# Up-projections in one stream: seven-product column groups in five pairs instead of one, and VectorE's placement copies on GpSimd

## The chip, the cores and the metric

The kernel runs on one core of a Trainium2 chip. The metric is the device time of one execution in microseconds. Five engines work in parallel, each through its own instructions in their order: TensorE (PE, with its weight loads as PEld), VectorE (DVE), ScalarE (ACT), GpSimd (POOL) and SyncE (SP), which issues nearly all loads of weights. Work on different engines meets at semaphores.

## The reference

A trunk of two layers on 256 positions of width 2048, all in float32. Layer 0 mixes positions with grouped-query attention, layer 1 with dilated window attention and a position bias. Each mixer is followed by a gated MLP, which is the part that the change touches most:

```python
def conv_ffn(h, w_up, conv_w, conv_b, w_down):     # D_FF = 5632
    u = h @ w_up                                   # 2048 -> 2 * 5632
    u = depthwise_conv3(u, conv_w) + conv_b        # along the positions
    gate, val = jnp.split(u, 2, axis=-1)
    return (jax.nn.silu(gate) * val) @ w_down      # 5632 -> 2048
```

(The convolution is written out here as a name; before each mixer and each MLP stands an RMS norm, behind each a residual add.)

## The kernel before

**Products.** All weights are float32. A block of a weight (`raw`, 128 rows by 2 x 512 columns, one load of 512 KB) is split by ScalarE into a rounded part `wh` and by VectorE into the rest `wl` (lines 130 and 131, in `split_raw`). The activations are split in the same way once. A product is then three matmuls: xh by wh, xl by wh, xh by wl. Every matmul that matters here has 512 columns. A regular unit of work (a "c unit") takes one block and both halves of the 256 positions: 2 row tiles x 2 halves x 3 = 12 matmuls.

**Seven products.** For some column groups (512 of the 2048 rows of the weight, over a pair of 512-column stripes), the 2 x 2 block product is made with seven products of sums of blocks instead of eight products of blocks. A "P unit" is one of those products: 2 row tiles x 3 = 6 matmuls, and it too needs one split of one block. Four regular c units (48 matmuls, four splits) become seven P units (42 matmuls, seven splits). Four of the seven products need a sum of weight blocks, and three or four of them a sum of activations, the "forms" (`make_forms`). The partial results M1, M5, M6, M7 are copied or added by ScalarE and VectorE into two tiles `ms`, and the results of the accumulators are added to them at the end.

**The MLP.** The 5632 columns are 11 stripes of 512 for the gate and 11 for the value; stripe p of both is a pair. Pairs 0 to 5 are the first half, 6 to 10 the second; each half is projected up and then at once down (`w_down` rows of that half), so a layer has up, down, up, down. `project` runs one stripe with four column groups of `feed` (16 c units a pair); pair 0 weaves its two stripes so that the last column groups of the input can still be made. Only the first pair of the second half (pair 6) goes through `seven`, with column group 0 as seven P units and the remaining twelve c units woven between. Its forms are made during the down-projection before it. In `feed` the second matmul of a block already reads `wl` (line 156 behind 155).

**Behind a stripe** runs the generator `up_post`: scale and copy out of PSUM (line 629), a 32 x 32 transpose on VectorE (630), sixteen copies that place the turned blocks (`place_blocks`, lines 395, 397 and 399; `PLACE = "pava"`: four on GpSimd, eight on ScalarE, four on VectorE), the convolution (638 to 644), then silu, the product with the gate and the splits (or forms) for the down-projection. A generator advances by one piece at each `step()`, which is called after each c unit; up to two generators advance at a time. The order of instructions on each engine is then set by a scheduler from the order of the code, in which the splits of weights are moved ahead by a fixed number of instructions (`AHEAD`).

**Buffers.** Six `raw` blocks, three pairs of `wh`/`wl` (four in the down-projection), eight PSUM banks. GpSimd issues the transfers that add one block onto another (`accum_op`), which the down-projection uses for one or two of its sums of blocks (line 251).

## Time and profile before

| | |
|---|---|
| median of 3 runs | 2234.61 us (2234.25 to 2234.72) |
| the profiled execution | 2234.03 us, its span 2232.2 us |
| TensorE busy | 2218.3 us, 99% |
| VectorE busy | 1848.1 us, 83% |
| ScalarE busy | 1564.8 us, 70% |
| GpSimd busy | 349.1 us, 16% |
| weight blocks split | 873 |

The busy time of TensorE is not the sum of its matmuls' durations: they overlap, one starting about every 0.227 us while each is shown with 0.39 us. What a matmul costs is therefore read from the distance of two starts, and a stall from a distance above it. By the first matmuls of each, the four stages of the MLP begin in layer 0 at 262.8 us (up), 526.3 (down), 650.3 (up) and 868.3 (down, to 974.4), and in layer 1 at 1514.8, 1777.2, 1901.1 and 2118.8 us (to the end).

### The profile page before, as it was taken

What the parts mean: (1) busy time and instruction counts of PE and PEld (TensorE: products, weight loads), DVE (VectorE), ACT (ScalarE), POOL (GpSimd) and SP (SyncE); (2) the same over time, 40 slices, a digit from 0 to 9 for tenths busy, and PEclk for the clock granted to TensorE, in tenths of its full rate; (3) what the DMA queues carried; (4) which work ended last, traced back from release to release, by engine and by line L of the source; (5) the groups of instructions that cost most, each with busy time, mean ns of one, the idle gap of its engine ahead of it and who ended that gap; (6) DMA issues with size and microseconds to landing.
All of it is one profiled execution on the core that took longest, in us unless ns stands there. A gap on an engine that the chain in (4) does not pass through costs nothing. (4 is left out here: it accounts for less than half of the span.)

```text
span 2232.2 us, 29276 instructions
## 1 busy us (share of the span) xinstructions
PE 2218.3 (99%) x9997; PEld 1834.7 (82%) x9997; DVE 1848.1 (83%) x2543; ACT 1564.8 (70%) x2411; POOL 349.1 (16%) x508
## 2 busy tenths in 40 slices
PE   9999999999999999999999999999999999999998
PEld 7888888888888888888888888888888888888886
DVE  6777778889998888879887978796887899888896
ACT  7665677777557777667876777575777765677764
POOL 2210212211001011111340213010111100011111
PEclk9999999999999999999999999999999999999999
DMA  8444657766776656766656565555666677566675
GB/s 302 163 148 151 204 189 210 242 200 193 235 217 205 199 193 193 246 204 205 214 176 191 167 207 179 189 197 185 196 193 194 199 226 227 199 197 191 222 236 161
DMA packets 129670, 448.99 MB, mean 201 GB/s; under 512 B 17664, under 2 KB 18432, under 8 KB 129520
## 3 DMA queue, kind: packets, MB, share of 16 engines
q1 hardware_dynamic: 119744, 425.64, 57.9%
q0 software_dynamic: 9344, 20.92, 4.9%
q8 instruction: 78, 1.28, 0.2%
q14 instruction: 72, 0.59, 0.1%
q10 hardware_dynamic: 432, 0.56, 0.1%
HBM read 438.11 MB, written 6.29 MB: 199 GB/s over the span
## 5 line engine op out<-in xcount | busy, mean ns | idle before, releaser
L131 DVE TENSOR_TENSOR wl<-raw,wh 128x1024 fp32r<-128x1024 f32 x873 | 1069.3, 1234 | 267.3 <-ACT wh L130 263.6
L130 ACT ACTIVATE wh<-raw 128x1024 fp32r<-128x1024 f32 x873 | 916.3, 1057 | 453.6 <-PE acc L157 157.6
L156 PE MATMUL acc<-wl,xh 128*128 128x512 f32 x1664 | 648.9, 390 | 1.4 <-DVE wl L131 0.9
L155 PE MATMUL acc<-wh,xh 128*128 128x512 f32 x1664 | 648.9, 390 | 0.5 <-ACT wh L166 0.5
L157 PE MATMUL acc<-wh,xh 128*128 128x512 f32 x1664 | 648.0, 389 | 0.0
L156 PEld LDWEIGHTS acc<-wl,xh 128*128 128x128 f32 x1664 | 312.5, 188 | 68.7 <-DVE wl L131 4.1
L155 PEld LDWEIGHTS acc<-wh,xh 128*128 128x128 f32 x1664 | 312.4, 188 | 64.7 <-ACT wh L166 0.9
L157 PEld LDWEIGHTS acc<-wh,xh 128*128 128x128 f32 x1664 | 312.4, 188 | 64.3
L320 PE MATMUL acc<-wh,ah 128*128 128x512 f32 x730 | 284.6, 390 | 0.4 <-DVE h L578 0.3
L322 PE MATMUL acc<-wh,al 128*128 128x512 f32 x730 | 284.3, 389 | 0.0
L395 POOL COPY u<-t 32x256 f32<-32x256 f32 x176 | 110.4, 627 | 805.3 <-DVE t L630 797.2
L325 PE MATMUL acc<-wl,ah 128*128 128x512 f32 x730 | 205.1, 390 | 0.6 <-DVE wl L131 0.6
L320 PE MATMUL acc<-wh,xh 128*128 128x512 f32 x416 | 162.9, 392 | 0.2 <-DVE h L578 0.2
L322 PE MATMUL acc<-wh,xh 128*128 128x512 f32 x416 | 162.0, 389 | 0.0
L320 PEld LDWEIGHTS acc<-wh,ah 128*128 128x128 f32 x730 | 137.0, 188 | 29.8 <-DVE h L578 1.3
L325 PEld LDWEIGHTS acc<-wl,ah 128*128 128x128 f32 x730 | 136.7, 188 | 30.2 <-DVE wl L131 2.0
L322 PEld LDWEIGHTS acc<-wh,al 128*128 128x128 f32 x730 | 137.1, 188 | 28.3
L397 ACT ACTIVATE u<-t 32x256 f32<-32x256 f32 x352 | 147.6, 419 | 17.2 <-DVE t L630 9.4
L325 PE MATMUL acc<-wl,xh 128*128 128x512 f32 x416 | 113.1, 390 | 0.0
L320 PEld LDWEIGHTS acc<-wh,xh 128*128 128x128 f32 x416 | 78.1, 188 | 16.8 <-DVE h L578 0.8
L325 PEld LDWEIGHTS acc<-wl,xh 128*128 128x128 f32 x416 | 78.0, 188 | 16.2
L322 PEld LDWEIGHTS acc<-wh,xh 128*128 128x128 f32 x416 | 78.1, 188 | 16.0
(271 smaller groups left out, 2487.1 us busy)
## 6 DMA issues: line engine op xcount, KB each, us to landing
raw<-in_w_up_dram SPq DMA_DIRECT2D x352, 512.0 KB, 4.5
raw<-in_w_down_dram SPq DMA_DIRECT2D x176, 512.0 KB, 5.0
raw<-in_w_b_dram SPq DMA_DIRECT2D x144, 512.0 KB, 4.5
raw<-in_w_bo_dram SPq DMA_DIRECT2D x48, 512.0 KB, 4.4
raw<-in_w_a_dram SPq DMA_DIRECT2D x40, 512.0 KB, 4.5
raw<-in_w_ao_dram SPq DMA_DIRECT2D x32, 512.0 KB, 3.7
raw<-in_w_down_dram POOLq DMA_DIRECT2D x17, 512.0 KB, 6.2
raw<-in_w_a_dram SPq DMA_DIRECT2D x16, 256.0 KB, 6.4
```

The source lines that it names most:

```text
L130: nc.scalar.activation(wh, r, AF.Copy)
L131: nc.vector.tensor_tensor(wl, r, wh.bitcast(F32), ALU.subtract)
L155: nc.tensor.matmul(accs[m], xh, wh[:, j, :], start=st, stop=False)
L156: nc.tensor.matmul(accs[m], xh, wl[:, j, :], start=False, stop=False)
L157: nc.tensor.matmul(accs[m], xl, wh[:, j, :], start=False, stop=sp)
L320: nc.tensor.matmul(acc[k], xh, wh[:, j, :], start=k in fresh, stop=False)
L322: nc.tensor.matmul(acc[k], xl, wh[:, j, :], start=False, stop=False)
L325: nc.tensor.matmul(acc[k], xh, wl[:, j, :], start=False, stop=last[k] == i and j == 1)
L395: nc.gpsimd.tensor_copy(dst, src)
L397: nc.scalar.activation(dst, src, AF.Copy)
```

## The change

The loops over the pairs of a half, `project`, `project_woven` and `seven` for one pair, are replaced by one function `stream`, which makes a list of units for all pairs of a half. Pairs 1, 3, 5, 7 and 9 (`SEVEN_UP`) take their column group 0 as seven P units, and these are woven between the last seven c units of the pair ahead of them. Pair 6 becomes a regular one. Of the four sums of weight blocks of such a group, two are made by VectorE (`add`) and two by transfers that GpSimd issues (`onto`). In a unit, the matmuls with `wh` (eight of a c unit, four of a P unit) all come ahead of those with `wl`. The forms are made at the start of each half (`half_forms`) and kept in tiles of the pools that the down-projection's inputs take later.

`PLACE` becomes `"papa"`: the four copies of VectorE go to GpSimd, which then has eight. `up_post` waits two steps more between the copies and the convolution. `bias_lines`, a side task of layer 0, gets other tiles, and one fixed PSUM bank for its six small matmuls.

**TensorE at the end of pair 0 in layer 0.** `acc` are accumulators in PSUM, `xh` activations, `fm` forms. Before, the value stripe of pair 0 ended, and pair 1 began, with c units one behind the other, each in the order wh, wl, wh:

```order
L155 MATMUL acc_2641<-wh_2876,xh_2430 128x512
L156 MATMUL acc_2641<-wl_2877,xh_2430 128x512
L157 MATMUL acc_2641<-wh_2876,xh_2430 128x512
L155 MATMUL acc_2642<-wh_2876,xh_2430 128x512
L156 MATMUL acc_2642<-wl_2877,xh_2430 128x512
L157 MATMUL acc_2642<-wh_2876,xh_2430 128x512
```

And with the change:

```order
L434 MATMUL acc_2785<-wl_2952,xh_2430 128x512
L434 MATMUL acc_2785<-wl_2952,xh_2433 128x512
L434 MATMUL acc_2786<-wl_2952,xh_2430 128x512
L434 MATMUL acc_2786<-wl_2952,xh_2433 128x512
L427 MATMUL acc_2973<-wh_2969,fm_2647 128x512
L428 MATMUL acc_2973<-wh_2969,fm_2648 128x512
L427 MATMUL acc_2973<-wh_2969,fm_2647 128x512
L428 MATMUL acc_2973<-wh_2969,fm_2648 128x512
L434 MATMUL acc_2973<-wl_2970,fm_2647 128x512 x2
L427 MATMUL acc_2785<-wh_2982,xh_2528 128x512
L428 MATMUL acc_2785<-wh_2982,xh_2528 128x512
```

A P unit of pair 1, with six matmuls on the form 2647/2648, now stands between two c units of pair 0, whose four matmuls with `wl` come at their end.

**VectorE where the two accumulators of a stripe with seven products are added to `ms`.** Before (pair 6, the value stripe), with the split `wl_6508` that is next:

```order
L131 TENSOR_TENSOR wl_6472<-raw_6446,wh_6471 128x1024
L642 SCALAR_TENSOR_TENSOR cg_6300<-u_2617,cw_2605,cg_6300 128x256 x2
L644 SCALAR_TENSOR_TENSOR cg_6300<-u_2617,cw_2605,cg_6300 128x256 x2
L425 TENSOR_TENSOR ms_6073<-acc_6076,ms_6073 128x512
L426 TENSOR_TENSOR ms_6073<-acc_6077,ms_6073 128x512
L131 TENSOR_TENSOR wl_6508<-raw_6503,wh_6507 128x1024
```

With the change (pair 1, the gate stripe):

```order
L132 TENSOR_TENSOR wl_3325<-raw_3322,wh_3324 128x1024
L762 SCALAR_TENSOR_TENSOR cv_2875<-u_2618,cw_2605,cv_2875 128x256
L797 TENSOR_TENSOR cv_2875<-cg_2873,cv_2875 128x512
L442 TENSOR_TENSOR ms_2886<-acc_2942,ms_2886 128x512
L442 TENSOR_TENSOR ms_2886<-acc_3116,ms_2886 128x512
L132 TENSOR_TENSOR wl_3350<-raw_3347,wh_3349 128x1024
```

The two adds stand in both directly ahead of a split, and wait for the end of a stripe; less of other work is ahead of them now, and there are ten such stripes a layer instead of two.

**GpSimd in the first pairs of layer 0.** `u` is the placed stripe, `scr` a scratch of the side task. Before:

```order
L1147 CAST lh<-rs 128x768
L395 COPY u_2617<-t_2871 32x8x32 x4
L395 COPY u_2618<-t_3029 32x8x32 x4
L395 COPY u_2617<-t_3229 32x8x32 x4
L395 COPY u_2618<-t_3433 32x8x32 x4
L1161 DMA scr_97<-lnt 4x32x512 x4
```

With the change:

```order
L1257 CAST lh_3688<-rs 128x128
L373 DMA raw_2884<-in_w_up_dram 128x1024
L511 COPY u_2617<-t_2877 32x8x32 x8
L373 DMA raw_2936<-raw_2967 128x1024
L511 COPY u_2618<-t_3107 32x8x32 x8
L511 COPY u_2617<-t_3275 32x8x32 x8
L511 COPY u_2618<-t_3445 32x8x32 x8
```

Eight copies where there were four, and the two adding transfers of pair 1 (line 373) now stand among them, the second behind the eight copies of a stripe.

The diff, cut to its core:

```diff
-PLACE = "pava"
+SEVEN_UP = (1, 3, 5, 7, 9)
+PLACE = "papa"
...
+    def stream(w, lhs, forms, pairs, is_seven, held, gate_done, value_done, new_sums):
+        units, left = [], {}
+        for p in pairs:
+            order = WOVEN if held and p == pairs[0] else [(c, k) for c in range(2) for k in range(4)]
+            if p in is_seven:
+                units[-7:] = [u for v, f in zip(units[-7:], ORDER_D) for u in (v, ("P", p, 0, f))]
+            units += [("c", p, k, 2 * c + i) for c, k in order for i in range(2) if k or p not in is_seven]
+            left.update({(p, n): 8 for n in range(2)})
+            if p in is_seven:
+                left.update({(p, 0): 8, (p, 1): 7})
+        sets = [(bank_at[0] + 2) % 4, bank_at[0]]
+        acc, sums, blocks = {}, {}, {}
+
+        def where(p, k):
+            if (p, k) not in acc:
+                n, m = {"11": (0, 0), "21": (0, 1), "12": (1, 0), "22": (1, 1)}.get(k, (None, None))
+                if n is None:
+                    i = {"M1": 4, "M5": 5, "M6": 6, "M7": 7}[k]
+                elif p in is_seven and n:
+                    i = 4 + m
+                else:
+                    i = sets[n] + m
+                acc[p, k] = bank(i, "acc")
+                return acc[p, k], True
+            return acc[p, k], False
+
+        def block(p, b):
+            if b not in blocks:
+                blocks[b] = load_raw(w, p + NPAIR * (int(b[1]) - 1), 0, int(b[0]) - 1)
+            return blocks[b]
+
+        def add(b, src):
+            with tc.high_priority(offset=AHEAD):
+                nc.vector.tensor_tensor(blocks[b], blocks[b], blocks[src], ALU.add)
+
+        def onto(b, src):
+            nc.gpsimd.dma_start(blocks[b].rearrange("p a c -> p (a c)"), src, accum_op=ALU.add)
+
+        def fetch(p, f):
+            if f == 1:
+                block(p, "11")
+                block(p, "12")
+            elif f == 2:
+                add("11", "12")
+                onto("12", w[p + NPAIR, 0][:, 1024:])
+            elif f == 5:
+                add("22", "11")
+                onto("21", block(p, "22").rearrange("p a c -> p (a c)"))
+            b = {1: "11", 2: "21", 3: "22", 5: "11", 6: "22", 7: "12", 4: "21"}[f]
+            return b, block(p, b)
+
+        def product_done(p, f):
+            (k0, k1), (q0, q1) = sums[p]
+            k = {1: "M1", 5: "M5", 6: "M6", 7: "M7"}[f]
+            t = acc.pop((p, k))
+            if f in (1, 5):
+                nc.scalar.activation(k0 if f == 1 else q1, t, AF.Copy)
+            elif f == 6:
+                nc.vector.tensor_tensor(q0, t, k0, ALU.add)
+            else:
+                nc.vector.tensor_tensor(k1, t, q0, ALU.add)
+                nc.vector.tensor_tensor(q0, q0, q1, ALU.add)
+                nc.vector.tensor_tensor(q1, k1, q1, ALU.add)
+
+        for i, (kind, p, kg, f) in enumerate(units):
+            if held and i == 2 * held:
+                drain()
+            if kind == "c":
+                b, r = None, load_raw(w, p + NPAIR * (f // 2), kg, f % 2)
+                n, ks = f // 2, (("11", "21"), ("12", "22"))[f // 2]
+            else:
+                b, r = fetch(p, f)
+                n = {2: 0, 4: 0, 3: 1}.get(f)
+                ks = ({1: "M1", 2: "11", 3: "12", 4: "21", 5: "M5", 6: "M6", 7: "M7"}[f],)
+                if f == 1:
+                    sums[p] = new_sums()
+            free = kind == "c" or f in (5, 6, 7, 4)
+            wh, wl = split_raw(r, free)
+            if kind == "P" and free:
+                blocks.pop(b)
+            todo = []
+            for j in range(2):
+                for m, k in enumerate(ks):
+                    if kind == "c":
+                        x = at(lhs[4 * kg + 2 * (f % 2) + j], m)
+                    else:
+                        x = forms[f]
+                        x = x[j] if isinstance(x, list) else [t[:, j * P:(j + 1) * P] for t in x]
+                    todo.append((*where(p, k), *x, j))
+            for t, fresh, xh, xl, j in todo:
+                nc.tensor.matmul(t, xh, wh[:, j, :], start=fresh, stop=False)
+                nc.tensor.matmul(t, xl, wh[:, j, :], start=False, stop=False)
+            todo.sort(key=lambda u: ([u[0] is acc[p, k] for k in ks].index(True), u[4]))
+            if n is not None:
+                left[p, n] -= 1
+            ends = n is None or left[p, n] == 0
+            for t, fresh, xh, xl, j in todo:
+                nc.tensor.matmul(t, xh, wl[:, j, :], start=False, stop=ends and j == 1)
+            if n is None:
+                product_done(p, f)
+            elif ends:
+                a = [acc.pop((p, k)) for k in (("11", "21"), ("12", "22"))[n]]
+                if p in is_seven:
+                    s = sums[p][n]
+                    for m in range(2):
+                        nc.vector.tensor_tensor(s[m], a[m], s[m], ALU.subtract if n else ALU.add)
+                    a = s
+                    if n:
+                        sums.pop(p)
+                        sets.reverse()
+                (gate_done, value_done)[n](a, p)
+            if kind == "c" or f in (1, 5, 7, 4):
+                step()
+        bank_at[0] = sets[1]
...
                 place_blocks(u.rearrange("p j (m t) -> p j m t", m=2), t, PLACE)
                 yield
+                yield
+                yield
                 for hh in range(2):
...
+            kept, up_forms = {}, ({}, {})
+
+            def form_tiles(hf):
+                fm = [tuple(wp.tile([P, NT], F32R, tag=f"a{c}{k}", name=nm("fm")) for c in "hl")
+                      for k in range(26 + 2 * hf, 30)]
+                if hf == 0:
+                    t = [wp.tile([P, 2, 512], F32, tag=t, name=nm("xs")).rearrange("p a c -> p (a c)")
+                         for t in ("wh9", "wl9")]
+                else:
+                    t = [t[:, :1024] for t in ut]
+                    f2 = fp.tile([P, 4, NT], F32R, tag="tT", name=nm("ff"))
+                    fm += [(f2[:, 0], f2[:, 1]), (f2[:, 2], f2[:, 3])]
+                return *(v.rearrange("p (j c) -> p j c", j=4) for v in t), fm
+
+            def half_forms(hf):
+                for _ in range(4 * hf):
+                    yield
+                yield from make_forms(up_forms[hf], hT, 0, partial(form_tiles, hf))
+                if hf:
+                    zero_edges()
...
+                def gate_done(a, p, hf=hf, p0=p0, slots=slots, forms=forms, new_form=new_form, cs=cs):
...
+                    cs[p] = [[fp.tile([P, 2, NT], F32, tag=t, name=nm(t), bufs=3) for _ in range(2)]
+                             for t in ("cg", "cv")]
+                    start(up_post(a, p, cs[p][0]))
...
+                def value_done(a, p, p0=p0, slots=slots, forms=forms, cs=cs):
+                    cg, cv = cs.pop(p)
...
-                    if hf == 1 and p == p0:
-                        sums = [wp.tile([P, 2, 512], F32, tag=t, name=nm("ms")) for t in ("wh9", "wl9")]
-                        c = [("c", k, 2 * n + i) for n in range(2) for k in kgs[1:] for i in range(2)]
-                        units = c[:2]
-                        for i, f in enumerate(ORDER):
-                            units += [("P", 0, f)] + c[2 + i:3 + i] * (i < 5)
-                        units += c[7:]
...
-                        seven(w_up[l], p, NPAIR + p, hT, lambda kg: first_forms, units,
-                              [[t[:, i] for i in range(2)] for t in sums], gate_ready, value_ready)
-                        continue
-                    cg, cv = new_tiles()
-                        va = project_woven(w_up[l], p, NPAIR + p, hT, WOVEN, 4, gate_done)
-                    else:
-                        start(up_post(project(w_up[l], p, hT, kgs), p, cg))
-                        va = project(w_up[l], NPAIR + p, hT, kgs)
+                    start(up_post(a, NPAIR + p, cv, after))
...
+                start(half_forms(hf))
+                stream(w_up[l], hT, up_forms[hf], range(p0, p1), SEVEN_UP, 4 * (hf == 0), gate_done, value_done,
+                       lambda: [[t[:, i] for i in range(2)] for t in
+                                [wp.tile([P, 2, 512], F32, tag=t, name=nm("ms")) for t in ("wh9", "wl9")]])
...
-                if hf == 0:
-                    start(first_half_forms())
...
+        oh = [wp.tile([P, NT], F32R, tag=f"a{c}{k}", name=nm("oh")) for k in (24, 25) for c in "hl"]
...
+            t = bank(7, "ps")
+            for j, i in enumerate(cols):
+                nc.tensor.matmul(t[:, j * NT:(j + 1) * NT], lh.rearrange("p a r -> p (a r)"), oh[i],
+                                 start=True, stop=True)
```

More of the change, by code (lines that the diff above doesn't have):

```diff
@@ L699, in glu_forms @@
                 put(3, s4)
-            kgs = list(range(4))
             for hf, (p0, p1) in enumerate(HALVES):
@@ L710, in ffn @@
                 wide.append(1)
-                for p in range(p0, p1):
+                cs = {}
+                def gate_done(a, p, hf=hf, p0=p0, slots=slots, forms=forms, new_form=new_form, cs=cs):
                     if p - p0 in SKG[hf]:
@@ L725, in ffn, with after @@
                         slots.update({4 * (p - p0) + j: new_form() for j in range(4)})
-                    def new_tiles():
-                        return ([fp.tile([P, 2, NT], F32, tag=t, name=nm(t), bufs=3) for _ in range(2)]
-                                for t in ("cg", "cv"))
-                    def after(hh, cg, cv, slots=slots, forms=forms, kg=p - p0):
+                    if p == 0:
+                        taps()
+                    cs[p] = [[fp.tile([P, 2, NT], F32, tag=t, name=nm(t), bufs=3) for _ in range(2)]
[3 more added lines that the diff above has]
+                    cg, cv = cs.pop(p)
+                    def after(hh, kg=p - p0):
                         if kg in forms:
@@ new lines, in bias_lines @@
+        of = lp.tile([P, 2, 512], F32, tag="tT", name="of").rearrange("p a c -> p (a c)")
+        oh = [wp.tile([P, NT], F32R, tag=f"a{c}{k}", name=nm("oh")) for k in (24, 25) for c in "hl"]
+        rb = lp.tile([P, 32], F32, name="rb")[:, :24]
+        rs = lp.tile([P, 32], F32R, name="rs")[:, :24]
+        nc.gpsimd.memset(rb, 0.0)
+        nc.gpsimd.memset(rb[32:33, :], -1e30)
+        for i in range(2):
+            nc.gpsimd.dma_start(of[64 * i:64 * i + 64], onehot[:64])
+            nc.gpsimd.dma_start(rb[64 * i:64 * i + 32, :], rel_bias)
```

70 lines of the change are left out of this document (20 added, 50 removed).

## The prediction, made before the changed kernel ran

> **What bounds the kernel now.** I read the page first, then the distances between starts on TensorE, then who keeps TensorE waiting, then the busy time of every engine stage by stage.
>
> ```profile
> span 2232.2 us, 29276 instructions
> PE 2218.3 (99%) x9997; PEld 1834.7 (82%) x9997; DVE 1848.1 (83%) x2543; ACT 1564.8 (70%) x2411; POOL 349.1 (16%) x508
> PEclk9999999999999999999999999999999999999999
> 299.95 0.39 PE L157 MATMUL acc<-wh,xh 128*128 128x512 f32 x1
> ...
> 305.85 0.39 PE L156 MATMUL acc<-wl,xh 128*128 128x512 f32 x1
> PEld acc L156 <- DVE wl L131: 4.1, 8, 0.8
> PEld acc L320 <- DVE h L578: 2.1, 4, 0.7
> PEld acc L325 <- DVE wl L131: 2.0, 4, 0.7
> ```
>
> The clock is full throughout. Between the two matmuls shown lie 26 starts: 5.90 / 26 = 0.227 us from one to the next. That is the cost of one matmul of 512 columns, not the 0.39 us that it is shown with. The last three rows are the largest waits of TensorE's weight loads over the whole span: 8.2 us. So the time is the number of matmuls times 0.227 us, and whoever wants a shorter time must remove matmuls without making TensorE wait. The other engines matter only through such waits.
>
> ```profile
> 262.80:526.30 263.50, 263.50 (x1171) 218.20 (x1170) 212.32 (x321) 195.13 (x302) 50.81 (x83) 1.00 0.68 211
> 526.30:650.30 124.00, 123.41 (x542) 101.18 (x541) 117.57 (x129) 77.01 (x90) 8.08 (x12) 1.00 0.75 224
> 650.30:868.30 218.00, 217.41 (x955) 178.72 (x954) 184.09 (x269) 161.59 (x248) 23.11 (x36) 1.00 0.61 197
> ```
>
> These are three stages of layer 0 (up, down, up). After the length come the busy times of PE, PEld, DVE, ACT and POOL. VectorE is busy for 81%, 95% and 84%, ScalarE for 74%, 62% and 74%. VectorE is thus the engine that can become late first, and its fullest stage is a down-projection with six groups of seven products, 42 P units.
>
> **What is removed: 48 matmuls.** Per pair and column group, four c units of 12 matmuls become seven P units of 6: 48 become 42. Each layer has five such pairs instead of one, so 2 x 4 x 6 = 48 matmuls go: 48 x 0.227 = 10.9 us. The side task's six small matmuls keep their columns (two of 512 become four of 256). No load of a weight goes or comes on SyncE's queue: the four blocks of the group are loaded once either way.
>
> **What is added on VectorE.** The groups that carry the prices:
>
> ```profile
> L131 DVE TENSOR_TENSOR wl<-raw,wh 128x1024 fp32r<-128x1024 f32 x873 | 1069.3, 1234 | 267.3 <-ACT wh L130 263.6 <-PE ps L521 0.5 <-issue 0.2
> L399 DVE COPY u<-t 32x256 f32<-32x256 f32 x176 | 64.7, 368 | 5.9
> L277 DVE TENSOR_TENSOR raw<-raw,raw 128x1024 f32<-128x1024 f32 x40 | 49.3, 1234 | 2.3 <-DMA raw<-in_w_up_dram 1.8
> L420 DVE TENSOR_TENSOR ms<-acc,ms 128x512 f32<-128x512 f32 x8 | 5.5, 684 | 0.0
> L130 ACT ACTIVATE wh<-raw 128x1024 fp32r<-128x1024 f32 x873 | 916.3, 1057 | 453.6 <-PE acc L157 157.6 <-PE acc L322 137.9 <-DMA raw<-in_w_down_dram 40.6
> L341 DVE TENSOR_TENSOR fm<-u,fm 128x256 fp32r<-128x256 f32 x4 | 1.7, 426 | 0.0
> ```
>
> A group of seven costs VectorE three more splits (3 x 1.234), two sums of blocks (2 x 1.234; the other two go to transfers), and eight adds of partial results (8 x 0.684): 11.6 us. The forms of a half are some twelve instructions of 256 columns, 12 x 0.426 = 5.1 us. What goes are four copies a stripe, 4 x 0.368 = 1.5 us. Up, first half: 3 x 11.6 + 5.1 - 12 x 1.5 = +21.9 us on 212.3, in a stage that is 4.1 us shorter: 90%. Second half: 11.6 more for the second group, 2.5 less for the two sums that pair 6 made on VectorE, 14.7 less for ten stripes: -5.6 us, 82%. ScalarE gets 3 x 1.057 and two copies of partial results a group and stays under 80%.
>
> Inside a woven stretch I compared more closely. From the first split of a P unit to the last stand 12 further splits (14.8 us), the two sums (2.5), four adds (2.7) and, by the order of VectorE in pairs 6 and 7, other work of about 3 us: 23 us, while TensorE has six c units and six P units, 108 matmuls or 24.5 us. For pair 1 the same count gives about 24 us against 23 to 24. So the stretches are nearly balanced, and not beyond what the down-projection does with 95%. There the weight loads waited for `wl` and for accumulators as follows (520 to 640 us, whose groups are the six):
>
> ```profile
> PEld acc L325 <- DVE wl L131: 1.0, 2, 0.7
> PEld acc L320 <- DVE h L578: 0.7, 1, 0.7
> ```
>
> 1.7 us for six groups, 0.28 us each. That is the price I take for each of the ten new groups: +2.8 us. The bounds: nothing at all, or what the old group of pair 6 cost in its place:
>
> ```profile
> 698.52 0.39 PE L155 MATMUL acc<-wh,xh 128*128 128x512 f32 x1
> 699.27 0.50 PE L156 MATMUL acc<-wl,xh 128*128 128x512 f32 x1 [0.36 <-DVE wl L131]
> 699.61 0.39 PE L157 MATMUL acc<-wh,xh 128*128 128x512 f32 x1
> ...
> 731.95 0.39 PE L155 MATMUL acc<-wh,xh 128*128 128x512 f32 x1
> 732.38 0.50 PE L156 MATMUL acc<-wl,xh 128*128 128x512 f32 x1
> 732.72 0.39 PE L157 MATMUL acc<-wh,xh 128*128 128x512 f32 x1
> 696.80 0.68 DVE L425 TENSOR_TENSOR ms<-acc,ms 128x512 f32<-128x512 f32 x1
> 697.40 0.68 DVE L426 TENSOR_TENSOR ms<-acc,ms 128x512 f32<-128x512 f32 x1
> 698.00 1.22 DVE L131 TENSOR_TENSOR wl<-raw,wh 128x1024 fp32r<-128x1024 f32 x1
> ```
>
> Distances of 0.75, 0.34, 0.43 and 0.34 instead of 0.227 are 0.95 us lost, once a layer. The cause is in the last rows: the two adds wait for the end of the stripe, and the split behind them is late, because the very next matmul of the new block reads `wl`. This group is dissolved: -1.9 us for both layers. In the new order the same adds stand ahead of a split, but eight matmuls with `wh` come first, so `wl` is due 7 x 0.227 = 1.6 us later than before. That covers the 0.5 us of the first stall, and is why I stay with the lower price. If this cover is not enough, all ten groups cost 0.95.
>
> **What moves to GpSimd.**
>
> ```profile
> L395 POOL COPY u<-t 32x256 f32<-32x256 f32 x176 | 110.4, 627 | 805.3 <-DVE t L630 797.2
> 722.36 2.77 POOL L395 COPY u<-t 32x256 f32<-32x256 f32 x4 [18.04 <-DVE t L630]
> 722.15 1.18 DVE L131 TENSOR_TENSOR wl<-raw,wh 128x1024 fp32r<-128x1024 f32 x1
> 723.25 1.16 DVE L341 TENSOR_TENSOR al<-st,ah 128x256 fp32r<-128x256 f32 x2
> 724.44 0.38 DVE L399 COPY u<-t 32x256 f32<-32x256 f32 x1
> 724.85 1.36 DVE L131 TENSOR_TENSOR wl<-raw,wh 128x1024 fp32r<-128x1024 f32 x1
> 726.24 0.28 DVE L399 COPY u<-t 32x256 f32<-32x256 f32 x1
> L251 POOL DMA_DIRECT2D raw<-in_w_down_dram x17 | 14.9, 876 | 188.5 <-DVE raw L255 79.8 <-ACT wh L130 73.8 <-DMA raw<-in_w_down_dram 34.9
> raw<-in_w_down_dram POOLq DMA_DIRECT2D x17, 512.0 KB, 6.2
> raw<-raw POOLq DMA_DIRECT2D x5, 512.0 KB, 6.6
> ```
>
> Eight copies take 8 x 0.627 = 5.0 us instead of 2.5, still behind each other and ahead of the convolution of the stripe. The two added steps, at one per c unit (12 x 0.227 = 2.7 us), give them 5.4 us; no one waits for the stripe until its column group is due in the down-projection, behind several c units and P units. Cost on the path: nothing, hidden by the next pair's matmuls; without that cover 2.5 us at the end of a half, four times. The rows at 722 show that the copies do slow VectorE: two instructions of 0.42 us took 1.16, a split 1.36 instead of 1.23, a copy 0.38 instead of the 0.28 of those beside no GpSimd work; together 0.56 us for four copies. Four more a stripe put 12 x 0.56 = 6.7 us on VectorE in the first half: 93%. This is at the level of the down-projection, whose price I use.
>
> [...]
>
> The transfers that add a block have GpSimd for issuer, so each stands behind any copies ahead of it. For the sum needed by product 7, from its issue at product 2 lie four c and four P units (16.3 us); copies, issue, landing and split take 5.0 + 0.9 + 6.2 + 2.3 = 14.4 us. For product 4 the way is three and three (12.2 us) against 14.8 us, if eight copies stand right ahead. VectorE works up to two units (4 us) ahead of TensorE, so even this is just in time, and in the order of GpSimd only pair 1 of each layer has the copies there. Cost taken: nothing; bound: 2.6 us a group.
>
> **The sum.** 2234.0 (the profiled execution) - 10.9 - 1.9 + 2.8 = 2224.0. The median of the three runs is 0.6 us above that execution, so 2224.6; I write 2224.5.
>
> **Rivals.** (1) *Every group stalls like the old one*: VectorE's adds still hold up the splits. 2234.6 - 10.9 - 1.9 + 10 x 0.95 = 2231.3. For it: the same adds ahead of the split, 90% in the first half. Against it: the 1.6 us, and the rows of the down-projection. (2) *The adding transfers come late*, in every group, as product 4 waits behind GpSimd's queue: 2234.6 - 12.8 + 10 x 2.6 = 2247.8, slower. It decides from 1.3 us a group. Against it: a lead of two units, and where the down-projection uses the same transfers they were not waited for by TensorE. (3) *GpSimd's copies stop VectorE for their whole length*: 22 stripes a layer x 4 x 0.627 = 55 us. The two up stages of a layer would need 396.4 + 21.9 - 5.6 + 55 = 468 us of VectorE, at the 95% that it reached at most 493 us, where they now last 481.5: 2234.6 + 2 x 11 = 2257. [...] The row of 1.36 us speaks against it.
>
> **Chances.** The forecast 0.77 (its own range 2221.5 to 2228), rival 1 0.15, rival 2 0.05, rival 3 0.03. The lower end is the sum without any new stall, 2221.8. The range reaches to rival 1, 2231: it leaves out rivals 2 and 3, half of rival 1 and a little of the forecast. A measurement of this kernel tells 0.2%, 4.5 us, from no change, so faster means under 2230.1: nearly all of the forecast and a third of rival 1, 0.82; same: the rest of rival 1 and little of 2, 0.11; slower 0.07.
>
> **What would show it.** TensorE's busy share stays at 99%, starts 0.227 us apart, and the up stages of a layer shorten by about 4 us in the first half and by 2 in the second; splits go from 873 to 897; VectorE's copies `u<-t` are gone and GpSimd has 352. Right about the stalls: TensorE's waits for `wl` in the up stages stay under 3 us for both layers, and none is for an adding transfer. Rival 1 shows as `wl` waits of about 1 us at the end of each stripe with seven products; rival 2 as ScalarE's `wh` waiting on a `raw` transfer from GpSimd, with TensorE behind it; rival 3 as splits of 1.6 us and more wherever GpSimd copies. The forecast is wrong if TensorE loses more than 0.8 us a group.

## The result

The changed kernel takes 2274.02 us (median, 2272.05 to 2275.1), the kernel before 2234.66 beside it: a ratio of 1.0175, 95% interval 1.0157 to 1.0192. It is slower by 39 us, where 10 us less were forecast. The page of its profiled execution has:

```profile
PE 2224.5 (98%) x9951; PEld 1828.8 (80%) x9951; DVE 1868.4 (82%) x2491; ACT 1582.4 (70%) x2457; POOL 487.8 (21%) x712
L132 DVE TENSOR_TENSOR wl<-raw,wh 128x1024 fp32r<-128x1024 f32 x897 | 1096.6, 1233 | 295.8 <-ACT wh L131 285.3
L511 POOL COPY u<-t 32x256 f32<-32x256 f32 x352 | 226.4, 643 | 597.8 <-DVE t L746 579.8
L434 PEld LDWEIGHTS acc<-wl,xh 128*128 128x128 f32 x1308 | 246.2, 189 | 52.7 <-DVE wl L132 1.6
```

The work is what was expected: 46 matmuls fewer in the count (48 of the groups less, two small ones of the side task more), 897 splits, 352 copies on GpSimd. VectorE is busy for 82%. What changed is TensorE's waiting. I summed by how much the distances between two starts exceed 0.227 us (those within 0.02 us of it left out): 16 us before, 66 us after, so 50 us of new stalls against 10.9 us of matmuls removed. The busy time by stage (length, then PE, PEld, DVE, ACT, POOL, the clock, the share of the DMA engines, GB/s) shows where: up, down, up of layer 0, then the same of layer 1.

```profile
262.30:539.40 277.10, 265.18 (x1155) 216.48 (x1154) 222.85 (x316) 202.09 (x319) 88.86 (x141) 0.98 0.70 209
539.40:671.40 132.00, 126.13 (x541) 101.96 (x540) 123.98 (x137) 78.40 (x90) 11.58 (x15) 0.99 0.74 221
671.40:892.00 220.60, 216.93 (x950) 177.19 (x949) 178.47 (x245) 162.59 (x254) 49.20 (x77) 1.00 0.64 200
1539.70:1805.50 265.80, 261.59 (x1147) 214.57 (x1146) 221.00 (x310) 201.53 (x319) 65.52 (x99) 0.99 0.64 200
1805.50:1936.60 131.10, 125.70 (x541) 102.00 (x540) 124.39 (x138) 78.83 (x90) 10.46 (x15) 0.99 0.74 222
1936.60:2157.30 220.70, 217.05 (x949) 177.08 (x948) 177.18 (x244) 162.21 (x254) 51.35 (x81) 1.00 0.65 203
```

In layer 0 the first up stage went from 263.5 to 277.1 us, the first down-projection, which the change does not touch, from 124.0 to 132.0, the second up stage from 218.0 to 220.6. No engine is full in any up stage: VectorE 80 to 83%, ScalarE 73 to 76%. So this is lateness, not load. The waits (total, times, longest) name who was late:

```profile
PEld acc L427 <- ACT wh L131: 34.2, 29, 5.8
PEld acc L326 <- DVE wl L132: 14.2, 11, 3.4
ACT wh L131 <- DMA raw<-in_w_up_dram: 24.7, 12, 8.4
ACT cg L756 <- POOL u L511: 13.4, 8, 1.7
ACT cv L756 <- POOL u L511: 12.0, 11, 2.0
```

Before, the largest waits of TensorE were for VectorE's `wl`. Now the largest by far is for ScalarE's `wh` in the up stages (L427), and ScalarE itself waited for loads and for GpSimd's copies. I followed the large stalls back one by one and found three kinds.

**First kind: the convolution waits for GpSimd, and a split waits behind the convolution.** The timeline of ScalarE, GpSimd and TensorE in the second up stage of layer 0 (start, length, engine, instruction; in brackets the idle time ahead of it and who ended it):

```profile
785.64 2.64 ACT L513 ACTIVATE u<-t 32x256 f32<-32x256 f32 x6 [0.60 <-DVE t L746]
785.67 6.27 POOL L511 COPY u<-t 32x256 f32<-32x256 f32 x8 [14.87 <-DVE t L746]
788.30 1.06 ACT L131 ACTIVATE wh<-raw 128x1024 fp32r<-128x1024 f32 x1
789.39 0.85 ACT L513 ACTIVATE u<-t 32x256 f32<-32x256 f32 x2
791.97 0.60 ACT L756 ACTIVATE cg<-u,cw 128x256 f32<-128x256 f32 x1 [1.73 <-POOL u L511]
792.48 1.04 ACT L131 ACTIVATE wh<-raw 128x1024 fp32r<-128x1024 f32 x1
793.57 0.50 PE L427 MATMUL acc<-wh,xh 128*128 128x512 f32 x1 [1.79 <-ACT wh L131]
```

ScalarE's eight copies and one split are done at 790.24; GpSimd's eight copies take 6.27 us and end at 791.94. The next `wh` stands behind the convolution in ScalarE's order and starts 0.51 us after it, at 792.48, so the convolution's wait of 1.73 us holds it back, and TensorE's next matmul starts 2.18 us after the start of the one before it instead of 0.227. The same picture stands at 1662.00 (2.20 us) and 2058.80 (2.19), and smaller in several other stripes.

**Second kind: a weight block arrives late.** Twice in the woven pairs of layer 0, where the side task stores to `scr` (timeline, then two rows on landings):

```profile
384.08 1.06 ACT L131 ACTIVATE wh<-raw 128x1024 fp32r<-128x1024 f32 x1 [5.45 <-DMA raw<-in_w_up_dram]
385.19 0.50 PE L427 MATMUL acc<-wh,xh 128*128 128x512 f32 x1 [3.87 <-ACT wh L131]
401.33 2.00 ACT L131 ACTIVATE wh<-raw 128x1024 fp32r<-128x1024 f32 x2 [8.36 <-DMA raw<-in_w_up_dram]
402.44 0.79 PE L427 MATMUL acc<-wh,xh 128*128 128x512 f32 x1 [5.38 <-ACT wh L131]
scr<-lnt POOLq DMA_DIRECT2D x8, 256.0 KB, 14.7
DMA to landing us min/median/max: 12.0/12.8/13.7
```

The last row is that of three weight loads and one adding transfer issued between 386 and 396 us; the row ahead of it gives the landing of the larger `scr` stores (before: 10.8 us). Distances of 4.26 and 5.77 us stand at the two starts. A group of seven holds four of the six `raw` buffers over many units, so the loads of the c units run with two buffers, and when one lands in 12 to 15 us instead of 4.6 (the page's median of the 352 loads of `w_up`), TensorE has nothing in hand.

**Third kind: VectorE at the end of pair 5.** This is the last pair of the first half, with a group of seven; behind it comes the down-projection:

```profile
542.49 1.28 DVE L442 TENSOR_TENSOR ms<-acc,ms 128x512 f32<-128x512 f32 x2
543.69 2.35 DVE L132 TENSOR_TENSOR wl<-raw,wh 128x1024 fp32r<-128x1024 f32 x2
546.09 1.22 PE L326 MATMUL acc<-wl,ah 128*128 128x512 f32 x3 [2.92 <-DVE wl L132]
```

TensorE needs the second of the two splits in the second row. It stands behind the two adds of the first row, which close pair 5's value stripe, and behind one other split, and comes 3.1 us too late (a distance of 3.31; in layer 1, at 1812.21, 3.35). The down-projection, with VectorE at 94%, has little to make this up, and distances of 1 to 1.6 us follow in it.

**What the stalls bring with them.** After some of them the matmuls start at half rate:

```profile
1662.00 0.50 PE L427 MATMUL acc<-wh,xh 128*128 128x512 f32 x1 [1.81 <-ACT wh L131]
...
1662.80 0.63 PE L428 MATMUL acc<-wh,xh 128*128 128x512 f32 x1
1663.23 0.63 PE L427 MATMUL acc<-wh,xh 128*128 128x512 f32 x1
1662.79:1666.20 3.41, 3.41 (x9) 2.65 (x8) 3.37 (x6) 3.41 (x6) 0.00 (x0) 0.50 0.94 210
```

From 1662.80 on eight distances in a row are 0.427 us, 1.6 us more than at 0.227; the last row, in the columns of the stage table, has a granted clock of 0.50 for that stretch. Seven or eight such distances in a row also follow the stalls at 402.44, 546.09 and 1812.21. The first row of the stage table has a clock of 0.98 where it was 1.00.

### The profile page after: what moved, and what is told of

Same layout as the page of the kernel before. It is cut to its first block, busy times and chain, and to the rows that moved or that the text cites. A ratio compares the mean times of both kernels' runs of the same rounds, so it can differ in the third digit from the quotient of the medians.

```text
span 2272.8 us, 29557 instructions
## 1 busy us (share of the span) xinstructions
PE 2224.5 (98%) x9951; PEld 1828.8 (80%) x9951; DVE 1868.4 (82%) x2491; ACT 1582.4 (70%) x2457; POOL 487.8 (21%) x712
## 3 DMA queue, kind: packets, MB, share of 16 engines
q8 instruction: 78, 1.28, 0.2%
## 5 line engine op out<-in xcount | busy, mean ns | idle before, releaser
L132 DVE TENSOR_TENSOR wl<-raw,wh 128x1024 fp32r<-128x1024 f32 x897 | 1096.6, 1233 | 295.8 <-ACT wh L131 285.3
L131 ACT ACTIVATE wh<-raw 128x1024 fp32r<-128x1024 f32 x897 | 935.3, 1055 | 444.2 <-PE acc L323 102.1
L427 PE MATMUL acc<-wh,xh 128*128 128x512 f32 x1308 | 514.6, 393 | 23.4 <-ACT wh L131 23.2
L428 PE MATMUL acc<-wh,xh 128*128 128x512 f32 x1308 | 511.5, 391 | 0.0
L511 POOL COPY u<-t 32x256 f32<-32x256 f32 x352 | 226.4, 643 | 597.8 <-DVE t L746 579.8
L434 PE MATMUL acc<-wl,xh 128*128 128x512 f32 x1308 | 353.9, 391 | 0.0
L427 PEld LDWEIGHTS acc<-wh,xh 128*128 128x128 f32 x1308 | 246.7, 189 | 85.1 <-ACT wh L131 34.2
L434 PEld LDWEIGHTS acc<-wl,xh 128*128 128x128 f32 x1308 | 246.2, 189 | 52.7 <-DVE wl L132 1.6
L428 PEld LDWEIGHTS acc<-wh,xh 128*128 128x128 f32 x1308 | 246.8, 189 | 50.1
L156 PE MATMUL acc<-wh,xh 128*128 128x512 f32 x384 | 150.6, 394 | 0.0
L157 PE MATMUL acc<-wl,xh 128*128 128x512 f32 x384 | 150.2, 391 | 0.3 <-DVE wl L132 0.2
L158 PE MATMUL acc<-wh,xh 128*128 128x512 f32 x384 | 150.0, 391 | 0.0
L321 PE MATMUL acc<-wh,xh 128*128 128x512 f32 x312 | 122.2, 392 | 0.0
L323 PE MATMUL acc<-wh,xh 128*128 128x512 f32 x312 | 121.5, 389 | 0.0
L157 PEld LDWEIGHTS acc<-wl,xh 128*128 128x128 f32 x384 | 72.2, 188 | 16.1 <-DVE wl L132 1.3
```

Of the source, the lines that this page charges most:

```text
L131: nc.scalar.activation(wh, r, AF.Copy)
L132: nc.vector.tensor_tensor(wl, r, wh.bitcast(F32), ALU.subtract)
L156: nc.tensor.matmul(accs[m], xh, wh[:, j, :], start=st, stop=False)
L157: nc.tensor.matmul(accs[m], xh, wl[:, j, :], start=False, stop=False)
L158: nc.tensor.matmul(accs[m], xl, wh[:, j, :], start=False, stop=sp)
L321: nc.tensor.matmul(acc[k], xh, wh[:, j, :], start=k in fresh, stop=False)
```

## The experiments

**The copies shared with VectorE again, the rest of the change kept.**

```diff
-PLACE = "papa"
+PLACE = "pava"
```

> The change with one part undone: the four copies a stripe are back on VectorE, all else stays. Theory T1: the stalls in the up stages come from ScalarE, whose convolution waits for GpSimd's eight copies (6.3 us in the profile of the change) with the next split of a weight queued behind it; then ScalarE's waits for GpSimd (25 us) go, the stalls of about 2.2, 1.5 and 1 us before the woven groups go with them, and the time falls by 8 to 14 us, to 2260 to 2266. Rival T2 (the weight blocks come late, because four of six are held by a group): the loads are as late as before, 2271 to 2275, or more, since VectorE has 65 us of copies again.

Measured: 2251.81 us (ratio to before 1.0083, 1.0068 to 1.0099), 22.2 us less than the change, more than expected. The three up stages whose only large stalls were of the first kind, the second of layer 0 and both of layer 1, are now:

```profile
666.10:882.30 216.20, 215.52 (x950) 177.68 (x949) 190.11 (x280) 162.80 (x254) 27.96 (x41) 1.00 0.64 204
1528.60:1788.40 259.80, 259.04 (x1146) 213.59 (x1145) 234.60 (x354) 201.60 (x319) 38.19 (x55) 1.00 0.66 204
1919.70:2135.90 216.20, 215.54 (x949) 177.60 (x948) 189.07 (x281) 162.43 (x254) 29.60 (x45) 1.00 0.65 207
```

4.4, 6.0 and 4.5 us shorter, and shorter than before the change (218.0, 262.4 and 217.7), although VectorE is now busier, 87 to 90% where it was 80 to 83%. The first up stage of layer 0 gave another 8.1 us (269.0 instead of 277.1). The order of ScalarE is the same, row for row, in this kernel and in the change, and at the place shown above nothing waits any more:

```profile
778.14 3.55 POOL L511 COPY u<-t 32x256 f32<-32x256 f32 x4 [16.82 <-DVE t L746]
781.87 0.85 ACT L513 ACTIVATE u<-t 32x256 f32<-32x256 f32 x2
782.80 0.60 ACT L756 ACTIVATE cg<-u,cw 128x256 f32<-128x256 f32 x1
783.31 1.04 ACT L131 ACTIVATE wh<-raw 128x1024 fp32r<-128x1024 f32 x1
```

**No groups of seven in the up stages; the stream, the order within a unit and the placement kept.**

```diff
-SEVEN_UP = (1, 3, 5, 7, 9)
+SEVEN_UP = ()
```

> The change without any group of seven products in the up stages: one stream, eight copies on GpSimd, two more steps. TensorE has 12 matmuls more than the kernel before (2.7 us). If the loss comes from weaving the groups (T2, and the order at the end of a half), it is 2235 to 2239 with stalls like before's. If the stream itself or GpSimd's copies cost by themselves (T1), ScalarE's waits for GpSimd stay and it is 2245 or more.

Measured: 2238.34 us (1.0019, 1.0009 to 1.0028). This kernel has 12 matmuls more than the one before (2.7 us) and not its two stalling groups (1.9), so 3.5 us are not accounted for by these. The up stages hardly stall (0.6 us in all four). So eight copies on GpSimd make ScalarE wait here too (23.4 us in all), but without woven groups that does not reach TensorE in the up stages. What is left over lies in the down-projections, which are 0.7 to 1.5 us longer each than before.

**Pair 5 without seven products.**

```diff
-SEVEN_UP = (1, 3, 5, 7, 9)
+SEVEN_UP = (1, 3, 7, 9)
```

> The change without the group of pair 5, the last of the first half. Theory T3: the first splits of the down-projection stand on VectorE behind the adds that wait for the end of pair 5's value stripe, and the first stage of the down-projection loses 7 to 8 us in each layer by that. Then both fall back to 124 to 125 us (from 132 and 131), the group's own stalls of 2.7 us go too, and 12 matmuls (2.7 us) come back: 2274 - 15 - 5 + 3 = 2257. If the longer down-projection has another cause (late blocks, forms), it stays at 130 to 132 us and the time at 2270 or more.

Measured: 2254.19 us (1.0087, 1.0069 to 1.0105), 19.8 us less than the change though it has 12 matmuls more. The down-projection behind it, in layer 0:

```profile
535.10:660.30 125.20, 123.70 (x542) 100.87 (x540) 116.56 (x124) 76.23 (x88) 11.24 (x15) 1.00 0.75 227
```

125.2 instead of 132.0 us, in layer 1 125.2 instead of 131.1, and no distance above 1.13 us is left in the stage shown: the group of pair 5 is what makes it late. That it does so by its two adds is read from the timeline. 4.2 and 1.7 us came from the first up stages too, whose last pair now runs ahead without a group.

**The side task left out (the position bias that it makes for layer 1 is zero).**

```diff
...
-    hT, ss = ffn(0, hT, ss, 2, False, bias_lines)
+    hT, ss = ffn(0, hT, ss, 2, False)
```

(In the lines at `...`, layer 1's bias tiles are filled with zeros in place of being loaded from `scr`.)

> The change without the side task in layer 0 and without the position bias that it makes for layer 1 (the bias is left at zero, so the output differs). The first up stage of layer 0 is 11 us longer than that of layer 1 in the profile of the change, with two stalls of 4.3 and 5.8 us where loads of weights took 12 to 15 us to land while the side task stored its lines. Theory T2: a group leaves two free blocks, so a slow load stops TensorE at once; without the stores the first up stage falls from 277 to 266 us and the time to about 2263. If the stores are not the cause, the stage stays over 274 us.

Measured: 2262.61 us (1.0128, 1.0112 to 1.0144), 11.4 us less than the change. All of it is in the first up stage of layer 0, 265.0 instead of 277.1:

```profile
262.50:527.50 265.00, 260.16 (x1147) 213.26 (x1146) 220.89 (x310) 201.84 (x319) 66.56 (x99) 1.00 0.64 201
```

The landings between 340 and 420 us, first of the change, then of this run, then of the run without groups of seven:

```profile
DMA to landing us min/median/max: 3.7/6.9/15.1
DMA to landing us min/median/max: 3.7/4.6/6.7
DMA to landing us min/median/max: 3.3/5.0/14.9
```

The last row shows that it takes both. Without groups of seven the side task still stores, and loads still land in up to 14.9 us, but TensorE is busy for all 263.6 us of that stage. So a slow load costs where a group holds the buffers. That the stores are what slows the loads, and not another part of the side task, is read from the timeline; they were not taken away alone.

**All three taken away at once.** The edits of the first, third and fourth run together; four groups of seven a layer remain.

> The three causes taken away at once: VectorE places half of the blocks again, pair 5 has no seven products, and the side task of layer 0 is left out (so no scratch stores; the position bias of the first attention is zero, and the output is not the reference's). The stream and four pairs of seven products a layer stay: 36 matmuls fewer than before, 36 x 0.227 = 8.2 us. If the three causes are all there is, each stage is as long as in the run that had its cause away: first halves about 261.2 us (pava's layer 1 plus six matmuls), second halves 216.2, down-projections 124 to 125.2 behind the first halves and as before behind the second: 2227 to 2230 us. If there is a fourth cause in the stream itself (a late weight load in every group, say), the up stages keep more than 10 us of stalls together and the time is 2236 or more.

Measured: 2226.08 us (0.9968, 0.9956 to 0.998), 48 us less than the change and 1 us better than the expectation's lower end. The up, down and up stages of layer 0, and TensorE's wait for `wh` in the up stages of the whole execution:

```profile
263.20:523.60 260.40, 260.07 (x1153) 214.85 (x1152) 231.32 (x353) 200.82 (x316) 36.10 (x53) 1.00 0.65 204
523.60:647.90 124.30, 123.16 (x541) 101.13 (x540) 118.39 (x129) 76.20 (x88) 8.77 (x11) 1.00 0.76 228
647.90:864.10 216.20, 215.53 (x949) 177.57 (x949) 190.13 (x280) 162.99 (x254) 28.04 (x41) 1.00 0.65 204
PEld acc L427 <- ACT wh L131: 4.3, 9, 1.2
```

No half rate (the clock is 1.00 in all three stages shown), and 3.5 us of stalls in the four up stages for eight groups, 0.44 us each. So no fourth cause of any size is left in the up stages. The single effects, 22.2 + 19.8 + 11.4 = 53.4 us, add up to more than the 47.9 us of all three, so some stalls had two causes.

**The two added steps: four, and none.** The change with `up_post` waiting for four steps, and for no step, between the block copies and the convolution.

```diff
                 place_blocks(u.rearrange("p j (m t) -> p j m t", m=2), t, PLACE)
                 yield
                 yield
                 yield
+                yield
+                yield
```

> The change with four added steps between the placing of the blocks and the convolution in place of two. If the copies on GpSimd cost because ScalarE's convolution comes to them too early and holds back the splits behind it, two more c units (about 5 us) let the copies end first: ScalarE's waits for POOL u fall below 3 us, the up stages come near those of the run with the copies shared (2252 to 2260 us). If the copies cost because they slow VectorE while they run, the extra steps change nothing: 2270 to 2276 us.

> The change without its two added steps. If the convolution's wait for GpSimd is what costs, the convolution now stands some 5 us nearer to the copies, nearly every stripe of the woven pairs makes ScalarE and with it TensorE wait: 2290 us or more. If the copies cost by slowing VectorE, the same copies run and the time stays 2270 to 2278 us.

Measured: 2266.98 us with four (1.0151, 1.0137 to 1.0165), 2271.73 with none (1.0167, 1.0153 to 1.0181). Both expectations of the first theory failed: four steps gain 7 us and not 14 to 22, none loses nothing. The waits of the first:

```profile
ACT cg L758 <- POOL u L511: 13.2, 8, 1.7
ACT cv L758 <- POOL u L511: 12.6, 12, 1.7
```

They are as in the change (without steps they are 29.7 us in all, where the change has 25.4). The reason is in the order of ScalarE: the steps hardly move the convolution against the splits. Counting `wh` between the last block copy of a stripe and its first convolution, in all 44 stripes, gives 40 in the change, 46 with four steps, 60 with none, never more than two in one stripe. The splits are issued with a priority of 45 instructions (`AHEAD`), and the scheduler weighs them against the copies by that; the rows of a stripe in the change show it (one of the roomier ones):

```
L513 ACTIVATE u_2618<-t_3968 32x8x32 x8
L131 ACTIVATE wh_4064<-raw_4062 128x1024
L131 ACTIVATE wh_4090<-raw_4088 128x1024
L756 ACTIVATE cv_3675<-u_2618,cw_2605 128x256 x2
```

So these two runs did not test the wait. A test had to change GpSimd's work and leave the orders alone.

**The placement alone, on the kernel without stalls; and on the kernel before.** The run with all three taken away, with `PLACE = "papa"` again; and the kernel before with `PLACE = "papa"` and the two steps.

> The run without the three causes, but GpSimd places eight blocks of a stripe again instead of four: the placement alone, on a kernel that otherwise hardly stalls (pair 5 without seven products, no side task, position bias zero). If the convolution's wait for GpSimd costs what the first pair of runs said (22 us from the change with shared placement to the change), and hardly depends on the other two causes: 2226 + 15 to 22 = 2241 to 2248 us, with TensorE's stalls behind ScalarE's waits for POOL u. If the causes only hurt together: below 2235.

> The kernel before with GpSimd placing eight blocks of a stripe and the two added steps, nothing else of the change. ScalarE's convolution waits for GpSimd here too, but the pairs are not woven and the splits run ahead: 2234 to 2237 us, if the wait reaches TensorE only where the split buffers are run empty by a group of seven. If the wait reaches TensorE by itself, in all 44 stripes: 2245 or more.

Measured: 2247.64 us (1.0061, 1.0046 to 1.0076), 21.6 us more than with shared copies, as much as in the change. On the kernel before: 2237.72 (1.0015, 1.0006 to 1.0024), 3.3 us more than the 2234.43 beside it. So eight copies on GpSimd cost 3.3 us where no group is woven into the pair ahead, about what the run without groups of seven had left over, and 22 us where groups are. On the kernel before, too, ScalarE waits 15.2 us for the copies, but no up stage is more than 0.1 us longer; 2.9 of the 3.3 us lie in the down-projections.

**Does GpSimd's work cost, or the wait for it?** On the run with all three taken away, GpSimd copies four blocks, and behind them makes four more copies of the same size that nobody reads. In the first form the new instructions also moved ScalarE's order. The second form:

```diff
+                at_p = tc.cur_priority
+                for i in range(4):
+                    nc.gpsimd.tensor_copy(idle[:32, :, :, :32], u.rearrange("p j (m t) -> p j m t", m=2)[:32, :, :, 96:128])
+                tc.cur_priority = at_p
                 for hh in range(2):
```

(The first form has the four copies at the end of `place_blocks`, and the priority counts them. In both, the tile `idle` is made ahead of `up_post`, and the edits of the run with all three taken away are in it.)

> The run without the three causes, VectorE placing four blocks of a stripe, and GpSimd four, but behind its own four GpSimd makes four more copies of the same size into a tile that nobody reads. GpSimd works as long as in the change, and its copies run beside VectorE as there; only nobody waits for the last four (side task left out, position bias zero). If eight copies cost because the convolution waits for them: 2226 to 2230 us. If they cost because GpSimd's copies slow VectorE, or hold up the transfers that GpSimd issues behind them: as the run with eight real copies, 2241 to 2248.

> The last test once more with nothing else moved. In the run with four idle copies the order of ScalarE had changed too: ScalarE's eight block copies stood in one row ahead of a split at places where a split stood among them. Here the orders of ScalarE, VectorE and SyncE are the same, row for row, as in the run without the three causes (VectorE places four blocks, GpSimd four, side task left out, position bias zero), and GpSimd makes four more copies of the same size behind its own four, which nobody waits for. If eight copies cost because ScalarE's convolution waits for the last of them: 2225 to 2229 us. If they cost by slowing VectorE or by holding up GpSimd's transfers: 2239 (the run with the changed order) to 2248 (eight real copies).

Measured: the first form 2239.25 us (1.0023, 1.0013 to 1.0032). ScalarE waits for no copy, and the 2.2 us stalls are gone, but new distances of 1.1 to 1.4 us come where ScalarE's eight copies now stand in one row ahead of a split. The second form, with the orders of ScalarE, VectorE and SyncE unchanged: 2232.73 (0.9992, 0.9982 to 1.0001), 6.7 us above the run with four copies and 14.9 below that with eight that are waited for. That lies between the two ranges expected (2225 to 2229, 2239 to 2248): neither account alone is enough. The same place in the run with eight real copies, and then in the second form:

```profile
771.12 0.60 ACT L756 ACTIVATE cg<-u,cw 128x256 f32<-128x256 f32 x1 [1.72 <-POOL u L511]
```

```profile
765.65 0.60 ACT L762 ACTIVATE cg<-u,cw 128x256 f32<-128x256 f32 x1
765.76 3.22 POOL L756 COPY idle<-u 32x256 f32<-32x256 f32 x4
L132 DVE TENSOR_TENSOR wl<-raw,wh 128x1024 fp32r<-128x1024 f32 x891 | 1088.1, 1232 | 221.4 <-ACT wh L131 207.5 <-PE acc L434 4.5 <-PE ps L719 3.0
L756 POOL COPY idle<-u x176: 391/396/1478, 296.1 to 2124.5; 32x256 f32<-32x256 f32 x176
```

The splits of the run with four copies:

```profile
L132 DVE TENSOR_TENSOR wl<-raw,wh 128x1024 fp32r<-128x1024 f32 x891 | 1084.8, 1228 | 227.3 <-ACT wh L131 218.6
```

GpSimd copies for as long as with eight real copies (228 us against 226), and the splits take 1232 ns against 1228 with four copies: 4 ns x 891 = 3.6 us. VectorE as a whole is busy for 1911.6 us against 1902.1, 9.5 us more. So of the 21.6 us some 15 go with the wait, and up to 7 with GpSimd's work beside VectorE. Two things are not held equal. With eight real copies VectorE places four blocks a stripe less, which can't be what makes that run slower. And the transfers that GpSimd issues go out behind all eight. ScalarE's waits for blocks of the up-projection are smaller there, though (4.1 us in all against 6.6 with idle copies), so late transfers don't explain the 15 us either.

**A version from what was found.** Shared copies, four groups of seven in layer 1, and in layer 0 only those of pairs 7 and 9, where the side task has ended.

```diff
+SEVEN_UP = ((7, 9), (1, 3, 7, 9))
+PLACE = "pava"
```

> A version meant to beat both, with the reference's whole computation: VectorE places half of the blocks again, pairs 1, 3, 7 and 9 have seven products in layer 1, in layer 0 only pairs 7 and 9 (where no scratch stores run). 24 matmuls fewer than before, 5.4 us. By the three causes: first half of layer 0 as without seven products (263.6 us), second halves 216.2, first half of layer 1 261.2, down-projections +1 each behind the first halves: 2229 to 2232 us. If the late weight loads by themselves cost more than the removed matmuls, 2234 or more.

Measured: 2231.11 us (0.9988, 0.9978 to 0.9997), as expected: 2.7 us faster than before, less than the 4.5 us that I call telling, but with its interval below 1.

## Why the prediction was wrong

**Right: what bounds the kernel, and the removed matmuls.** Each removed group saves six starts of 0.227 us: the second up stages with shared copies are 216.2 us with two groups each, where the kernel before, with the one stalling group, had 218.0 and 217.7. The -10.9 us are in the change too; 50 us of stalls lie over them.

**Right, with a small miss: the price of a group by VectorE's load.** 0.28 us a group was the estimate; the run with the three causes away has 0.44, with VectorE at 88 to 89%. Rival 1, a stall of 0.95 us in every group, did not come. VectorE's load in the up stages did not decide anything: the run with the three causes away is the fastest, and in it VectorE does more. The sum for that load was itself too high in the first half: +21.9 us forecast, +10.5 measured in layer 0 (212.3 to 222.85), for 90% and a measured 80%; in the second half it came out (178.5 and 178.47). The sign that the prediction set for the stalls, `wl` waits under 3 us in the up stages, came true as well (L434 waited 1.6 us for `wl`, the last row of the page above): it watched VectorE, and the stalls came through ScalarE's `wh`.

**Wrong: "Cost on the path: nothing, hidden by the next pair's matmuls", and that the two steps give the copies 5.4 us.** This is the step that failed most, 22 us. Three things were off. The steps do not separate the copies from the convolution in ScalarE's order, and this could be seen in that order beforehand: zero to two splits, about 0 to 2 us of ScalarE, not 5.4. The eight copies took 6.27 us, 0.78 each, not the 0.627 of the group's mean. And "no one waits for the stripe until its column group is due" looked only at who reads the result in the end; it left out that the convolution waits on ScalarE, in front of splits that TensorE needs at once. In the kernel before, four copies (2.77 us in the rows of the prediction) run beside ScalarE's own eight (8 x 0.42 = 3.4 us) and end first; eight do not.

**Wrong: "eight matmuls with `wh` come first, so `wl` is due 1.6 us later" as cover for the adds.** It holds between two pairs (1.6 us of waits for `wl` at L434 in the whole execution). Behind pair 5 there is no next pair but the down-projection, with another split between the adds and the one that is needed, and VectorE at 94%: 3.1 us, and 6 to 7 us with what follows, in each layer.

**Wrong: that the loads need no term.** "The four blocks of the group are loaded once either way" counts transfers, not buffers. Held for many units, four of six leave two for the rest; with the side task's stores that cost 11.4 us, without them 0.8 to 0.9 us behind a group (distances of 1.07 at 779.60 and 1.13 at 2026.57 in the run with the three causes away). I read the latter as the same shortage. A load lands 0.11 us ahead of ScalarE's late split there (778.39 and 778.50), as at the stalls above, but the profile puts the wait down to a matmul that ends in between, so this is not shown. A seventh buffer would tell; it was not tried.

**Rival 2** had the right place, late blocks in the groups, and the wrong transfers. ScalarE's waits for adding transfers were 12.0 us in the change and 10.5 in the run with the three causes away, which hardly stalls, and all of them lie in the down-projections; the late ones at 384.08 and 401.33 are plain loads.

**Rival 3** had the wrong size. It charged VectorE the mean of a copy, 0.627 us, for all 88 copies more in a layer: 55 us. No run shows such a loss. The test with idle copies adds 176 in both layers, and VectorE is busy for 9.5 us more. The row of these copies says why: half of them take 396 ns or less, the longest 1478. 45 of the 176 take over 0.7 us, and every one of these overlaps a split. So I read most of what the mean holds above 0.40 us as time that GpSimd's copies lose beside splits, not time that VectorE loses. The trace of the change has the same picture. A copy takes 0.40 us in the median where it overlaps no split (227 copies) and 1.28 where it overlaps one (125). A split takes 1.35 us in the median where it overlaps such a copy (86 splits) and 1.22 where GpSimd runs nothing beside it (675): 0.13 us, as in the prediction's row (1.36 instead of 1.23). What holds the two engines up there is not shown.

**Left open:** why four added steps gain 7 us with unchanged waits for GpSimd; and how the 6.7 us of the idle copies divide between longer VectorE instructions and transfers that GpSimd issues later.

## What to carry to other kernels

When work moves to a slower engine (here 0.627 us a copy on GpSimd against 0.368 on VectorE), ask in which engine's order the instruction stands that reads it, and what stands behind that instruction: the price here, 22 us, was that of the splits behind, not of the result. Count in the order of the instructions what lies between producer and consumer, since a step or a yield in the source need not keep them apart where splits carry a priority (60 splits in 44 stripes with no step, 40 with two, 46 with four). And read a buffer's holding time like an engine's load: here a group that keeps four of six buffers left the loads no slack for a slow transfer (distances of 4.26 and 5.77 us).

## What the hardware showed that was not expected

TensorE fell to half rate after a stall of only 2.20 us (1662.00), for eight matmuls of 0.427 us, but after two others of nearly the same length (2.18 at 793.57 and 2.19 at 2058.80) it did not. In the trace's clock records, up to 2260 us, half the clock lasts 3.41 us each time (6.83 at 399.86), and the starts (386.20, 399.86, 546.63, 1662.79 and 1812.98) lie whole multiples of 3.413 us apart: the later ones 4, 47, 374 and 418 of them behind the first. In the run with shared copies a distance of 3.31 us (540.47) has no slow stretch behind it, and one of 2.88 (569.51) has. So in these traces it is not the length of a stall alone that counts. What else does is left open. In the change these stretches are one more price of a stall, about 1.6 us each on top (eight distances of 0.427 us instead of 0.227).

GpSimd's copy of a 32x256 block took 0.62 us on average as an idle copy behind the others (3.22 us for four in a woven stretch), 0.64 in the change over all stripes, and 0.78 in the stripe shown. Behind these means stand two kinds: the median in the change is 0.402 us, and the 1.28 us of a copy beside a split (322.39 in the second form, with the split from 322.06 to 323.41) are three times that. So a mean over all stages understated what the copies cost in a stripe where they meet splits.
